# A decoder step whose second feed-forward takes its tokens as 256 and 320, with cache copies moved behind the weight loads

## The chip, the cores and the metric

The kernel runs on one core of a Trainium2 chip. The metric is the time of one execution in device microseconds; the median of three runs of the kernel before is 1784.57 us (1784.05 to 1786.42).

## What is computed

One layer of a hybrid decoder, for 1024 prompt tokens and 64 sample tokens (8 sequences of 8, each with 2048 cached rows of keys and values). Everything is float32.

```python
h = rmsnorm(x, norm_mix);  proj = h @ w_in                      # 1024 -> 3592
o_a = gated delta rule (4 heads of 128) on conv+silu of proj    # scratch mix, mixs[0]
o_b = dilated window attention (8 heads of 64)                  # prompt: own keys; sample: cache
x = x + concat(o_a, o_b) @ w_out                                # 1024 -> 1024
x = x + (silu(rmsnorm(x) @ w_gate) * (rmsnorm(x) @ w_up)) @ w_down   # 1024 -> 2816 -> 1024
y = rmsnorm(x, norm_final)
new_wk_sample = concat(cache_win_k, k)[:, 8:];  new_wv_sample = concat(cache_win_v, v)[:, 8:]
```

A sample query reads the cache at three strides: the last 512 rows (called near here), and before them rows 16 apart, of which 8 in every 16 are used, 96 groups of them (called far). The last line is a shift of the two caches by 8 rows: 8 x 2040 rows of 2 KB each, for keys and for values.

## The kernel before

Tokens stand in two groups: group 0 is 512 prompt tokens, group 1 the other 512; the 64 sample tokens go with group 0 up to attention and with group 1 from the second half of the output projection on (576 tokens then). Products of large matrices are made in three parts: an operand is split into a high part, rounded to a shorter float (`split`, L223 on ScalarE), and a low part, the rest (L224 on VectorE), and TensorE sums high x high, low x high and high x low (`mm`, L198).

A weight block of 0.5 MB is loaded by `wload` (L228, on the queue of the SyncE engine, SP) into one of `WB` = 2 buffers `wraw`; `wsplit` makes `whi` and `wlo` of it (three buffers each), or, where `own` is given, two tiles `own` of the caller's pool. `w_in`, `w_gate` and `w_up` are read as columns of 128 of the row-major matrix, runs of 512 B; `w_down` and `w_out` as runs of 1 or 2 KB.

The stages, in order of time: input norm and transposes (`norm_T`, L289 the scaled row, L294 the transposes; `wmix` is the norm's weight broadcast to all partitions, `ident` a part of the table `tab`), then `proj_a` and `proj_b` for both groups with the delta rule (`gdn`) beside them; first cache scores (`decode_k`), attention of group 0, and `outproj_a` (the half of the output projection that the delta rule feeds). Then the dense chain of group 0, `outproj_b(0)`, `ffn_norm(0)`, `ffn(0)`, runs beside three other works in turn: attention of group 1 (`attn(1)`), the rest of `decode_k`, and `decode_v` (cache values). At last comes the dense chain of group 1, `outproj_b(1)`, `ffn_norm(1)`, `ffn(1)`, which has nothing beside it but copies.

The work of a stage is written as generators that yield an estimate of their time, and `beside` takes steps of a side generator in proportion; a scheduler then orders each engine's instructions. What stands in an engine's order, or in a DMA queue, runs in that order.

`ffn` makes hidden blocks of 128 columns: `dense_T` for gate and for up (8 x 3 matmuls on `n` tokens each), tanh and product into `hh` and `hl`, and after 2 or 4 blocks the down product (`down`, `nat_mm`), which adds into `x2` (L1320). In `ffn(1)` the tokens stand as two pieces of 288; in `ffn(0)` as one of 512. The down product is 512 columns wide in `ffn(1)` and in the two-block step of `ffn(0)`, and 256 wide in the five four-block steps of `ffn(0)`. `outproj_b` works in four column pieces of 256 (L1238).

`decode_v` takes the sequences in pairs: the exponentials `Pd` (128 rows of both sequences by 616 columns) are transposed into `PT`, split into the tile `Z` at places that depend on the column group, and per sequence six loads `vt` (four far ones of 96 x 1024, two near ones of 128 x 1024, L1105) are split and multiplied: 26 matmuls of 512 columns a sequence.

The shifted caches are written in four ways. For keys: the near rows by eight copies of 1 MB from cache to output on the queue of GpSimd (POOL, L1026), written in `decode_k`; half of the far rows out of the loaded tile `kt` (L1039), half by `far_rows` (L1343), eight copies of 1.5 MB on SP beside `proj_b(0)`. For values: near and half of the far rows out of `vt` on POOL (L1108, L1110), the other half by `far_rows` beside the last dense chain.

Of the kernel before, what the change touches and what calls it, by code (L numbers as in the profile page):

```python
# [11 lines left out]
F32 = mybir.dt.float32  # L12
# [10 lines left out]
DB, DS = 8, 8  # L23
# [63 lines left out]
def consts():  # L87
# [6 lines left out]
    t["ident"] = p == c  # L94
# [43 lines left out]
    return off, {"table": table, "wb": wb, "dbias": np.ascontiguousarray(db_all), "xin": xin}  # L138


def laid_out(cache_k):

    k = cache_k[0, :, PAST - 512:].reshape(DB, 128, 4, 4, 128)
    return np.ascontiguousarray(k.transpose(0, 4, 3, 2, 1).reshape(DB, 128, 4, 512))


def body(tc, I, O, C, off):
# [25 lines left out]
    ident, ii, utri, ones = K("ident"), K("ii"), K("utri"), K("ones")  # L173
# [52 lines left out]
    def wload(src, k, n):  # L226
        raw = wp.tile([128, k, n], F32, name="wraw", tag="wraw", bufs=WB)
        sp.dma_start(raw, src)  # L228
        return raw

    def wsplit(src, k, n, raw=None, own=None):
        raw = wload(src, k, n) if raw is None else raw
        if own is None:
            hi = wp.tile([128, k, n], F32R, name="whi", tag="whi", bufs=WH)
            lo = wp.tile([128, k, n], F32R, name="wlo", tag="wlo", bufs=WL)
        else:
            hi, lo = (own.tile([128, k, n], F32R, name=f"own{q}", bufs=4) for q in range(2))
        split(hi, lo, raw)
        return hi, lo
# [80 lines left out]
    w_in = I["w_in"].rearrange("o (k p) n -> p (o k) n", p=128)  # L320
# [3 lines left out]
    def in_cols(i):  # L324
        return w_in[:, :, i * 128:(i + 1) * 128]
# [16 lines left out]
    def proj_a(G, tp, tb, hi, lo, ready={}):  # L342
# [38 lines left out]
        sp.dma_start(raw, w_in[:, :, 2048:2056])  # L381
# [35 lines left out]
    def proj_b(G, tp, hi, lo):  # L417

        W = GW[G]
        for kind in range(4):  # L420
            for j in range(4):
                c0_ = 2056 + kind * 512 + j * 128 if kind < 3 else 1536 + j * 128
                w = wsplit(w_in[:, :, c0_:c0_ + 128], 8, 128)
# [567 lines left out]
    def decode_k(tp, pairs, kb=2, kt_=3, qb=2, pb=1):  # L991
# [23 lines left out]
        for pi in pairs:  # L1015
            S = tp.tile([96, 2, 64], F32, name="S", tag="S", bufs=1)
            pa = obank()
            for s in range(2):
                b = 2 * pi + s
                c16, o16, c4, o4, src = cache_rows(I["cache_win_k"], O["new_wk_sample"], b)  # L1020
                for j in range(4):
                    for i in range(2):
                        hs = slice(i * 64, i * 64 + 64)
                        nc.gpsimd.tensor_copy(qbd[hs, s, j, 2 * j + i::8], qf[hs, j, b * 8:(b + 1) * 8])
                n = PAST - 512
                pool_q.dma_start(O["new_wk_sample"][0, b, n - DS:PAST - DS].rearrange("(a e) h d -> a (e h d)", a=64),  # L1026
                                 I["cache_win_k"][0, b, n:PAST].rearrange("(a e) h d -> a (e h d)", a=64))
# [31 lines left out]
    def decode_v(tp):  # L1059
# [6 lines left out]
        z = tp.tile([128, 13, 128], F32R, name="Z", bufs=1)  # L1066
        dve.memset(z.bitcast(F32), 0.0)
        X = tp.tile([128, 8, 64], F32, name="Xo", bufs=1)
        yield 3.0
        for pi in range(4):  # L1070
# [7 lines left out]
            pt = tp.tile([128, 6, 128], F32, name="PT", bufs=1)  # L1078
            p_ = abank()
            pe.transpose(p_[:96, 0:128], P[:, 0:96], ident)  # L1080
            pe.transpose(p_[:64, 128:256], pn, ident)
            act.activation(pt[:96, 0], p_[:96, 0:128], AF.Copy)
            act.activation(pt[:64, 1], p_[:64, 128:256], AF.Copy)
            p_ = abank()
            for i in range(4):
                pe.transpose(p_[:, i * 128:(i + 1) * 128], P[:, 96 + i * 128:224 + i * 128], ident)
            act.activation(pt[:, 2:6], p_.rearrange("p (i n) -> p i n", i=4), AF.Copy)
            for s in range(2):
                b = 2 * pi + s
                c = slice(s * 64, s * 64 + 64)  # L1090
                put = []
                for o in (0, 64):
                    put.append([bass.AP(tensor=z.tensor, offset=z.offset + o, ap=[[z.ap[0][0], 96], [136, 8], [1, 8]]),
                                z[:, 8:12, o:o + 64], z[:64, 12, o:o + 64]])
                srcs = [pt[:96, 0, c].rearrange("p (t h) -> p t h", t=8), pt[:, 2:6, c], pt[:64, 1, c]]
                for hi_, lo_, src_ in zip(*put, srcs):
                    split(hi_, lo_, src_)
                c16, o16, c4, o4, src = cache_rows(I["cache_win_v"], O["new_wv_sample"], b)
                po = obank()
                for i in range(6):  # L1100
                    n = 96 if i < 4 else 128
                    vt = tp.tile([128, 2, 512], F32, name="vt", tag="vt", bufs=TB)
                    vh = tp.tile([128, 2, 512], F32R, name="vh", bufs=VB)
                    vl = tp.tile([128, 2, 512], F32R, name="vl", bufs=VB)
                    sp.dma_start(vt[:n], c16[:96, 2 * i:2 * i + 2] if i < 4 else c4[:, 2 * i - 8:2 * i - 6])  # L1105
                    split(vh[:n], vl[:n], vt[:n])
                    if i < 4:
                        pool_q.dma_start(o16[0:95, 8 + 2 * i:10 + 2 * i], vt[1:96])  # L1108
                    else:
                        pool_q.dma_start(o4[:, 2 * i - 8:2 * i - 6], vt)  # L1110
                    for q in range(2):
                        mm(po, z[:n, 2 * i + q], vh[:n, q], i + q == 0, False)
                        mm(po, z[:n, 2 * i + q], vl[:n, q], False, False)
                    yield 2.5
                mm(po, z[:64, 12], vnh, False, False)
                mm(po, z[:64, 12], vnl, False, True)
# [28 lines left out]
    w_g = I["w_gate"].rearrange("o (k p) n -> p (o k) n", p=128)  # L1145
    w_u = I["w_up"].rearrange("o (k p) n -> p (o k) n", p=128)
    w_d = I["w_down"].rearrange("o (k p) n -> p (o k) n", p=128)
# [72 lines left out]
    def outproj_b(F, tp, x2):  # L1220
# [11 lines left out]
        for c in range(4):  # L1232
            w = wsplit(w_out[:, 4:8, c * 256:(c + 1) * 256], 4, 256)
            for i, rows, col in toks(F):
                ps = mbank()[:, :256]
                nat_mm(his(hi), his(lo), w, 4, rows, col, ps, True, True)
                xv = x2[:, col // 128, c * 256:(c + 1) * 256]
                dve.tensor_tensor(xv, ps, xv, op=OP.add)  # L1238
                yield 1.3
# [21 lines left out]
    def ffn(F, tp, x2, hp):  # L1261
        cols = [(0, 288), (288, 288)] if F else [(0, 512)]
# [19 lines left out]
        while f < nf:  # L1282
# [3 lines left out]
            for j in range(nb):  # L1286
                wg = wsplit(w_g[:, :, (f + j) * 128:(f + j + 1) * 128], 8, 128)
                wu = wsplit(w_u[:, :, (f + j) * 128:(f + j + 1) * 128], 8, 128)
                for c0, n in cols:
                    pg = yield from dense_T(*wg, hi, lo, c0, n)  # L1290
                    pu = yield from dense_T(*wu, hi, lo, c0, n)
                    th = hp.tile([128, 512], F32, name="hth", bufs=2)[:, :n]
                    act.activation(th, pg[:, :n], AF.Tanh, scale=0.5)  # L1293
                    dve.scalar_tensor_tensor(th, th, 1.0, pg[:, :n], op0=OP.add, op1=OP.mult)
                    dve.tensor_tensor(th, th, pu[:, :n], op=OP.mult)
                    act.activation(hh[j][:, c0:c0 + n], th, AF.Copy, scale=0.5)
                    m = min(n, 512 - c0)
                    dve.scalar_tensor_tensor(hl[j][:, c0:c0 + m], th[:, :m], 0.5, hh[j][:, c0:c0 + m].bitcast(F32),
                                             op0=OP.mult, op1=OP.subtract)
                    if m < n:  # L1300
                        dve.scalar_tensor_tensor(hh[j][:, 576:640], th[:, m:n], 0.5, hh[j][:, 512:576].bitcast(F32),
                                                 op0=OP.mult, op1=OP.subtract)
                yield 0.1
            last, wide = f + nb == nf, F or nb == 2
            ncol = 512 if wide else 256
            parts = nb * ncol // 1024

            def weights(c):

                k = nb // parts  # L1310
                return [wsplit(w_d[:, f + q * k:f + (q + 1) * k, c * ncol:(c + 1) * ncol], k, ncol, own=hp if F else None)
                        for q in range(parts)]
# [25 lines left out]

    def far_rows(c, o, new):
# [5 lines left out]
        sp.dma_start(o[0, :, PAST - DS:PAST].rearrange("b t h d -> b t (h d)"), new.rearrange("(b t) f -> b t f", t=DS))  # L1345

# [148 lines left out]
    far.run()  # L1495
# [28 lines left out]
```

## Time and profile before

| | before |
|---|---|
| median of three runs | 1784.57 us |
| the profiled execution | 1786.49 us |
| its span, first to last instruction | 1784.7 us |
| its mean granted TensorE clock | 0.981 of full speed |
| TensorE busy | 1697.0 us, 95% |
| VectorE busy | 1150.2 us, 64% |
| DMA | 324.96 MB, 182 GB/s over the span |

The profiled execution is 1.92 us above the median. Busy time counts the time from a matmul's start to its modelled end, and matmuls overlap, so that what one costs in a full stream is the distance from its start to the next start, not the duration in its row. The full clock is 2.4 GHz; a granted clock of 0.5 is 1.2 GHz.

### The profile page before, as it was taken

The page shows a single profiled execution, that of the slowest core. Times are in us where ns is not written, and L with a number is a line of the kernel's source. Part 1 is how long each engine was busy: PE and PEld are TensorE (multiplying, and loading weights), DVE is VectorE, ACT ScalarE, POOL GpSimd, SP SyncE. Part 2 cuts the span into 40 slices and gives each one's busy share as a digit, 9 for nine tenths or more (in the row PEclk, how much of TensorE's full clock was granted, in tenths as well). Part 3 has the DMA queues.
Part 4 walks back from the last instruction along what each step waited for, and adds up shares of the span by engine and source line. Part 5 has one row for each costly group of instructions (what it writes and reads, how often), then busy time and mean ns, then how long its engine had stood idle before and what let it go on. Part 6 is the DMA issues. An engine that isn't in the chain of part 4 may idle for free. (4 is left out here: it accounts for less than half of the span.)

```text
span 1784.7 us, 27958 instructions
## 1 busy us (share of the span) xinstructions
PE 1697.0 (95%) x10462; PEld 1464.7 (82%) x10462; DVE 1150.2 (64%) x2829; ACT 679.4 (38%) x1379; POOL 78.2 (4%) x200
## 2 busy tenths in 40 slices
PE   4999999997999999999999989999998999999997
PEld 4988789996766668878887778888887999999996
DVE  6978966866776757797666546676576444343435
ACT  4545434441423353676421134454234223131222
POOL 1000000001001000000011001111100000000000
PEclk9999999998999999999998999999998999999999
DMA  8645556468898867534299678798494333241321
GB/s 272 182 145 159 162 179 171 116 200 271 266 282 256 256 208 225 188 104 118 66 284 287 180 224 256 248 304 274 133 325 154 128 95 95 59 130 36 107 72 65
DMA packets 309569, 324.96 MB, mean 182 GB/s; under 512 B 28221, under 2 KB 260669, under 8 KB 307754
## 3 DMA queue, kind: packets, MB, share of 16 engines
q1 hardware_dynamic: 297754, 275.64, 51.6%
q0 software_dynamic: 10304, 43.08, 6.8%
q10 hardware_dynamic: 1376, 4.46, 0.7%
q8 instruction: 82, 1.34, 0.3%
q14 instruction: 53, 0.43, 0.1%
HBM read 251.31 MB, written 105.63 MB: 200 GB/s over the span
## 5 line engine op out<-in xcount | busy, mean ns | idle before, releaser
L198 PE MATMUL pm<-act_hi,whi 128*128 128x288 f32 (+1 forms) x1056 | 349.4, 331 | 0.2 <-ACT act_hi L223 0.2
L198 PE MATMUL pm<-act_lo,whi 128*128 128x288 f32 (+1 forms) x1056 | 348.1, 330 | 0.0
L198 PE MATMUL pm<-act_hi,wlo 128*128 128x288 f32 (+1 forms) x1056 | 347.4, 329 | 0.0
L223 ACT ACTIVATE whi<-wraw 128x1024 fp32r<-128x1024 f32 x182 | 192.8, 1059 | 381.8 <-PE pm L198 275.8
L224 DVE TENSOR_TENSOR wlo<-wraw,whi 128x1024 fp32r<-128x1024 f32 x182 | 222.3, 1222 | 123.8 <-ACT whi L223 123.3
L198 PE MATMUL pm<-xh,whi 128*128 128x320 f32 (+2 forms) x672 | 230.6, 343 | 11.5 <-ACT whi L223 8.6
L198 PE MATMUL pm<-xl,whi 128*128 128x320 f32 (+2 forms) x672 | 228.4, 340 | 0.1
L198 PE MATMUL pm<-xh,wlo 128*128 128x320 f32 (+2 forms) x672 | 226.7, 338 | 0.2
L198 PEld LDWEIGHTS pm<-act_hi,whi 128*128 128x128 f32 x1056 | 199.2, 189 | 18.4 <-issue 2.1
L198 PEld LDWEIGHTS pm<-act_hi,wlo 128*128 128x128 f32 x1056 | 199.3, 189 | 14.5 <-issue 0.5
L198 PEld LDWEIGHTS pm<-act_lo,whi 128*128 128x128 f32 x1056 | 199.3, 189 | 14.2 <-issue 0.2
L198 PEld LDWEIGHTS pm<-xh,whi 128*128 128x128 f32 x672 | 129.1, 192 | 25.9 <-ACT whi L223 9.1
L1320 DVE TENSOR_TENSOR x<-pm,x 128x256 f32<-128x256 f32 (+1 forms) x148 | 79.9, 543 | 98.2 <-PE pm L198 97.8
L198 PEld LDWEIGHTS pm<-xl,whi 128*128 128x128 f32 x672 | 129.0, 192 | 11.9 <-issue 3.2
L198 PEld LDWEIGHTS pm<-xh,wlo 128*128 128x128 f32 x672 | 128.7, 192 | 10.6 <-DVE wlo L224 1.5
L198 PE MATMUL pm<-own,hh 128*128 128x512 f32 x440 | 129.4, 390 | 0.0
L198 PE MATMUL pm<-whi,hh 128*128 128x256 f32 (+1 forms) x336 | 101.6, 303 | 12.9 <-DVE x L1320 7.6
L198 PE MATMUL pm<-whi,hl 128*128 128x256 f32 (+1 forms) x336 | 99.7, 299 | 0.0
L198 PE MATMUL pm<-wlo,hh 128*128 128x256 f32 (+1 forms) x336 | 99.4, 297 | 0.0
L198 PEld LDWEIGHTS pm<-own,hh 128*128 128x128 f32 x440 | 82.2, 188 | 16.9 <-issue 0.2
L198 PE MATMUL pm<-whi,nat_hi 128*128 128x256 f32 x288 | 83.4, 293 | 1.5 <-DVE n_ss L219 1.1
L1293 ACT ACTIVATE hth<-pm 128x288 f32<-128x288 f32 (+1 forms) x66 | 30.5, 462 | 139.4 <-PE pm L198 139.3
(362 smaller groups left out, 3180.9 us busy)
## 6 DMA issues: line engine op xcount, KB each, us to landing
wraw<-w_in SPq DMA_DIRECT2D x56, 512.0 KB, 4.6
wraw<-w_gate SPq DMA_DIRECT2D x44, 512.0 KB, 3.7
wraw<-w_up SPq DMA_DIRECT2D x44, 512.0 KB, 3.8
wraw<-w_down SPq DMA_DIRECT2D x44, 512.0 KB, 3.6
new_wk_sample<-cache_win_k SPq DMA_DIRECT2D x8, 1536.0 KB, 8.2
qbc<-smp SPq DMA_DIRECT2D x32, 384.0 KB, 7.2
kt<-cache_win_k SPq DMA_DIRECT2D x32, 384.0 KB, 7.0
vt<-cache_win_v SPq DMA_DIRECT2D x32, 384.0 KB, 4.2
```

The source lines that it names most:

```text
L198: pe.matmul(out, lhsT, rhs, start=start, stop=stop)
L223: act.activation(hi, src, AF.Copy)
L224: dve.tensor_sub(lo, src, hi.bitcast(F32))
L1293: act.activation(th, pg[:, :n], AF.Tanh, scale=0.5)
L1320: dve.tensor_tensor(xv, ps, xv, op=OP.add)
```

## The change

Seven edits.

1. The host lays the weights out in blocks, so that each of the 0.5 MB loads of `w_in`, `w_gate`, `w_up` and `w_down` reads 4 KB in one run per partition.
2. `ident` is loaded as a table of its own, behind `wmix`, and the rest of the table behind the five input tiles.
3. `move` issues one copy of 0.5 MB from cache to output on SP behind each weight load, as long as there are any. 16 such copies of near key rows start with the dense chain of group 0 and replace the eight of POOL; 64 of value rows (255 rows each, the whole shifted cache) start with the dense chain of group 1 and replace `far_rows` and the stores out of `vt`.
4. The far values come packed by the host, 128 rows full, three loads instead of four; the far exponentials are masked per residue and transposed as six full blocks, so that a sequence takes five loads and 22 matmuls, and a pair of sequences 11 transposes instead of 6. `Z` needs no clearing.
5. `outproj_b` works in two column pieces of 512, each with two loads of 0.5 MB.
6. All down products are 512 wide.
7. `ffn(1)` takes its tokens as 256 and 320. Its first two hidden blocks are made on the first 256 tokens, then on the other 320; the second block's weights go into `own` tiles meanwhile, with raw buffers (`raw2`) of their own.

```diff
+    moves = iter(())
+    def move():
+        x = next(moves, None)
+        if x is not None:
+            tc.keep_in_program_order(sp.dma_start(*(y.rearrange("s h d -> s (h d)") for y in x)))
+        return x
 def wload(src, k, n):
     raw = wp.tile([128, k, n], F32, name="wraw", tag="wraw", bufs=WB)
     sp.dma_start(raw, src)
+    move()
 def wsplit(src, k, n, raw=None, own=None):
+    if own is not None:
+        raw = own.tile([128, k, n], F32, name="raw2", bufs=2)
+        sp.dma_start(raw, src)
+        move()
...
-        return w_in[:, :, i * 128:(i + 1) * 128]
+        return I["w_in"][i]
...
 def decode_k(...):
-                pool_q.dma_start(O["new_wk_sample"][0, b, n - DS:PAST - DS]..., I["cache_win_k"][0, b, n:PAST]...)
...
 def decode_v(...):
-                for i in range(6):
+                for i in range(5):
-                    sp.dma_start(vt[:n], c16[:96, 2 * i:2 * i + 2] if i < 4 else c4[:, 2 * i - 8:2 * i - 6])
-                    split(vh[:n], vl[:n], vt[:n])
-                    if i < 4:
-                        pool_q.dma_start(o16[0:95, 8 + 2 * i:10 + 2 * i], vt[1:96])
-                    else:
-                        pool_q.dma_start(o4[:, 2 * i - 8:2 * i - 6], vt)
+                    sp.dma_start(vt, C["far_v"][b, i] if i < 3 else c4[:, 2 * i - 6:2 * i - 4])
+                    split(vh, vl, vt)
...
 def outproj_b(F, tp, x2):
-        for c in range(4):
-            w = wsplit(w_out[:, 4:8, c * 256:(c + 1) * 256], 4, 256)
+        for c in range(2):
+            w = [wsplit(w_out[:, k:k + 2, cs], 2, 512) for k in (4, 6)]
...
 def ffn(F, tp, x2, hp):
-        cols = [(0, 288), (288, 288)] if F else [(0, 512)]
+        cols = [(0, 256), (256, 320)] if F else [(0, 512)]
-            for j in range(nb):
+            early = F and f == 0
+            for j, (c0, n) in ([(j, c) for c in cols for j in range(nb)] if early else [(j, c) for j in range(nb) for c in cols]):
+                    ws[j] = [wsplit(I[x][f + j], 8, 128, own=hp if early and j else None) for x in ("w_gate", "w_up")]
-            last, wide = f + nb == nf, F or nb == 2
-            ncol = 512 if wide else 256
+            last, ncol = f + nb == nf, 512
...
     x0 = list(load_in(0, npl, range(2)))
-    sp.dma_start(tab, C["table"])
     wbc = bcast_row(npl, I["norm_mix"], "wmix")
+    sp.dma_start(ident, C["ident"])
     raws = [(i, wload(in_cols(i), 8, 128)) for i in IN_ORDER[:E1]]
     x0 += load_in(0, npl, range(2, 5))
+    sp.dma_start(tab, C["table"])
...
+    move_all(rows_of("cache_win_k", "new_wk_sample", PAST - 512, PAST, 256))
...
+    move_all(rows_of("cache_win_v", "new_wv_sample", DS, PAST, 255))
...
-    far = Side(far_rows(I["cache_win_v"], O["new_wv_sample"], smp[2]))
-    beside(out1, (far, 0.3))
-    beside(Side(ffn(1, op, x2, hp)), (far, 0.3))
+    beside(out1)
+    run(ffn(1, op, x2, hp))
```

Three places of the engines' orders show what these edits move. The first is the start of POOL's order, before and then changed; `gdn_S`, `Bz` and `N` are tiles of the delta rule.

```order
L1423 MEMSET gdn_S 128x512
L1026 DMA new_wk_sample<-cache_win_k 16x16384 x3
L1433 MEMSET Bz 128x1024
L1434 MEMSET N_1431 128x512
L1026 DMA new_wk_sample<-cache_win_k 16x16384 x3
```

```order
L1465 MEMSET gdn_S 128x512
L1475 MEMSET Bz 128x1024
L1476 MEMSET N_1433 128x512
L693 COPY N_1433<-L 32x4x32
L694 COPY N_1433<-L 32x4x32
```

The key copies, three of them right behind the first clearing, are gone from POOL. The second place is TensorE's order between `outproj_b(1)` (`nat_hi` its operand) and `ffn(1)` (`act_hi`, `act_lo` its operands, transposed from `xn`), before and then changed.

```order
L198 MATMUL pm<-wlo,nat_hi 128x256
L294 MATMUL pn<-tab,xn 128x128 x24
L198 MATMUL pm<-act_hi,whi 128x288 x2
L294 MATMUL pn<-tab,xn 128x128 x4
L198 MATMUL pm<-act_lo,whi 128x288
```

```order
L223 MATMUL pm<-wlo,nat_hi 128x512
L333 MATMUL pn<-ident,xn 128x128 x16
L223 MATMUL pm<-act_hi,whi 128x256
L223 MATMUL pm<-act_lo,whi 128x256
L223 MATMUL pm<-act_hi,wlo 128x256
```

A token tile of 128 has 8 transposes. Three tiles stood ahead of the first product, now two do; after 24 matmuls of 256 columns come the 16 transposes of tiles 2 and 3, after 14 more the 8 of the sample tile. The third place is SP's order at the start of `ffn(1)`, before and then changed; `wffn` and `wfin` are norm weights.

```order
L300 DMA wffn<-norm_ffn 128x1024
L1343 DMA new_wv_sample<-cache_win_v 96x4096
L228 DMA wraw<-w_gate 128x8x128
L228 DMA wraw<-w_up 128x8x128
L1343 DMA new_wv_sample<-cache_win_v 96x4096 x2
L228 DMA wraw<-w_gate 128x8x128
```

```order
L339 DMA wffn<-norm_ffn 128x1024
L253 DMA wraw<-w_gate 128x1024
L263 DMA new_wv_sample<-cache_win_v 16x8160
L253 DMA wraw<-w_up 128x1024
L263 DMA new_wv_sample<-cache_win_v 16x8160
L339 DMA wfin<-norm_final 128x1024
L269 DMA raw_13361<-w_gate 128x1024
```

A copy stands behind each of the first 58 of the 66 loads of `ffn(1)`; the other six of the 64 stand behind the two last loads of `ffn(0)` and the four of `outproj_b(1)`. SP's order up to attention of group 1 is otherwise the same as before, but for the table's place.

## Rows read from the trace of the kernel before

**Rows 1.** The page's part 1: busy us (share of the span) and count.
```profile
PE 1697.0 (95%) x10462; PEld 1464.7 (82%) x10462; DVE 1150.2 (64%) x2829; ACT 679.4 (38%) x1379; POOL 78.2 (4%) x200
```

**Rows 2.** Windows: us, busy (count) of each engine, granted clock, DMA share, GB/s.
```profile
0.00:18.00 18.00, 0.00 (x0) 0.00 (x0) 3.38 (x23) 3.58 (x5) 2.41 (x8) 1.00 0.89 318
...
884.00:902.00 18.00, 18.00 (x148) 17.72 (x148) 11.24 (x29) 3.74 (x4) 2.64 (x14) 1.00 0.61 177
...
900.00:1000.00 100.00, 93.17 (x482) 75.09 (x481) 63.77 (x80) 19.13 (x23) 13.96 (x43) 0.91 0.96 281
1040.00:1130.00 90.00, 82.10 (x439) 69.32 (x438) 52.62 (x78) 37.10 (x52) 10.86 (x22) 0.98 0.86 262
...
1316.00:1336.00 20.00, 20.00 (x172) 20.00 (x170) 15.63 (x44) 6.47 (x9) 0.00 (x0) 1.00 1.01 374
1336.00:1355.00 19.00, 10.11 (x50) 8.72 (x49) 17.75 (x49) 10.14 (x17) 0.95 (x1) 0.64 0.47 155
1362.00:1775.00 413.00, 413.00 (x2679) 388.58 (x2677) 181.57 (x315) 102.99 (x157) 0.00 (x0) 1.00 0.29 89
```

**Rows 3.** Timelines of DVE, POOL and SP at the start: start us, us, instruction.
```profile
17.23 1.28 DVE L289 SCALAR_TENSOR_TENSOR xn<-xt,n_ss,wmix 128x1024 f32<-128x1024 f32 x1 [8.97 <-DMA wmix<-norm_mix]
...
1.30 1.68 POOL L1026 DMA_DIRECT2D new_wk_sample<-cache_win_k  x3
...
1.66 0.43 SPq L1413 DMA_DIRECT2D tab<-table  x1
2.13 0.43 SPq L300 DMA_DIRECT2D wmix<-norm_mix  x1
```

**Rows 4.** Timeline of PE at the start.
```profile
23.05 0.56 PE L198 MATMUL pm<-xh,whi 128*128 128x256 f32 x1
...
28.02 1.65 PE L294 MATMUL pn<-tab,xn 128*128 128x128 f32 x12
...
34.45 1.09 PE L294 MATMUL pn<-tab,xn 64*128 64x64 f32 x8 [3.75 <-DVE n_ss L214]
```

**Rows 5.** Groups of PE by line and form: count | busy us, mean ns | idle before.
```profile
L198 PE MATMUL pm<-whi,hh 128*128 128x256 f32 x320 | 94.8, 297 | 12.8 <-DVE x L1320 7.6 <-DVE hth L1295 5.2
...
L198 PE MATMUL pm<-whi,nat_hi 128*128 128x256 f32 x288 | 83.4, 293 | 1.5 <-DVE n_ss L219 1.1 <-DVE xq L1210 0.3
```

**Rows 6.** Timeline of PE: streams of one form, first and last row.
```profile
904.64 0.39 PE L198 MATMUL pm<-act_hi,wlo 128*128 128x512 f32 x1
...
907.82 0.39 PE L198 MATMUL pm<-act_lo,whi 128*128 128x512 f32 x1
...
1335.76 0.28 PE L198 MATMUL pm<-wlo,nat_hi 128*128 128x256 f32 x1
...
1336.47 0.28 PE L198 MATMUL pm<-wlo,nat_hi 128*128 128x256 f32 x1
```

**Rows 7.** Timeline of PE: two transposes of `decode_v` with one matmul of 256 columns between them.
```profile
1169.41 0.27 PE L1080 MATMUL pa<-tab,Pd 128*96 128x128 f32 x1
...
1169.64 0.27 PE L1081 MATMUL pa<-tab,pn 128*64 128x128 f32 x1
```

**Rows 8.** Waits of SP's queue: us in total, times, longest; and PE's gap at 1061.
```profile
SPq L1105 <- DMA new_wv_sample<-vt: 45.6, 14, 8.6
...
1065.10 0.58 PE L198 MATMUL pm<-whi,hh 128*128 128x256 f32 x1 [3.85 <-DVE x L1320]
```

**Rows 9.** Timeline of PE between `outproj_b(1)` and `ffn(1)`.
```profile
1348.06 1.94 PE L294 MATMUL pn<-tab,xn 128*128 128x128 f32 x8 [3.39 <-DVE n_ss L216]
...
1353.40 0.59 PE L198 MATMUL pm<-act_hi,whi 128*128 128x288 f32 x1
```

**Rows 10.** The page's part 6, DMA issues: count, KB each, median us to landing.
```profile
wraw<-w_gate SPq DMA_DIRECT2D x44, 512.0 KB, 3.7
...
new_wv_sample<-cache_win_v SPq DMA_DIRECT2D x8, 1536.0 KB, 8.7
...
wb<-wb SPq DMA_DIRECT2D x8, 512.0 KB, 3.8
```

More of the change, by code (lines that the diff above doesn't have):

```diff
@@ L93, in consts @@
     t = {}
-    t["ident"] = p == c
     t["ii"] = (p % 64) == (c % 64)
@@ L171, in K @@
         return tab[:, o:o + n]
-    ident, ii, utri, ones = K("ident"), K("ii"), K("utri"), K("ones")
+    ident = cp.tile([128, 128], F32, name="ident")
+    ii, utri, ones = K("ii"), K("utri"), K("ones")
     hmask, bmask = K("hmask"), K("bmask")
@@ L1087, in decode_v @@
-            act.activation(pt[:, 2:6], p_.rearrange("p (i n) -> p i n", i=4), AF.Copy)
+            pf = tp.tile([128, 8, 96], F32, name="Pfar", bufs=1)
+            dve.tensor_tensor(pf, P[:, None, 0:96].to_broadcast([128, 8, 96]),
+                              bmask[:, :, None].to_broadcast([128, 8, 96]), op=OP.mult)
+            pfv = pf.rearrange("p t m -> p (t m)")
+            blocks = [pfv[:, k * 128:(k + 1) * 128] for k in range(6)]
+            blocks += [P[:, 96 + i * 128:224 + i * 128] for i in range(4)] + [pn]
@@ new lines, in decode_v @@
+            z = tp.tile([128, 11, 2, 2, 64], F32R, name="Z", bufs=1)
+            for k0 in range(0, 11, 4):
+                p_ = abank()
+                for k in range(k0, min(k0 + 4, 11)):
+                    n = 128 if k < 10 else 64
+                    pe.transpose(p_[:n, (k - k0) * 128:(k - k0 + 1) * 128], blocks[k], ident)
+                pv = p_.rearrange("p (k s n) -> p k s n", k=4, s=2)
+                if k0 < 8:
+                    split(z[:, k0:k0 + 4, :, 0], z[:, k0:k0 + 4, :, 1], pv)
+                else:
+                    split(z[:, 8:10, :, 0], z[:, 8:10, :, 1], pv[:, 0:2])
+                    split(z[:64, 10, :, 0], z[:64, 10, :, 1], pv[:64, 2])
@@ L1088, in decode_v @@
             for s in range(2):
                 b = 2 * pi + s
[L1090 to L1097, printed above, removed]
+                zk = [z[:, k, s].rearrange("p a n -> p (a n)") for k in range(11)]
@@ new lines, in ffn @@
+            ws = {}
+            for j, (c0, n) in ([(j, c) for c in cols for j in range(nb)] if early else [(j, c) for j in range(nb) for c in cols]):
+                if j not in ws:
+                    ws = ws if early else {}
+                    ws[j] = [wsplit(I[x][f + j], 8, 128, own=hp if early and j else None) for x in ("w_gate", "w_up")]
+                wg, wu = ws[j]
+                pg = yield from dense_T(*wg, hi, lo, c0, n)
+                pu = yield from dense_T(*wu, hi, lo, c0, n)
+                th = hp.tile([128, 512], F32, name="hth", bufs=2)[:, :n]
+                act.activation(th, pg[:, :n], AF.Tanh, scale=0.5)
+                dve.scalar_tensor_tensor(th, th, 1.0, pg[:, :n], op0=OP.add, op1=OP.mult)
+                dve.tensor_tensor(th, th, pu[:, :n], op=OP.mult)
+                act.activation(hh[j][:, c0:c0 + n], th, AF.Copy, scale=0.5)
+                m = min(n, 512 - c0)
+                dve.scalar_tensor_tensor(hl[j][:, c0:c0 + m], th[:, :m], 0.5, hh[j][:, c0:c0 + m].bitcast(F32),
+                                         op0=OP.mult, op1=OP.subtract)
+                if m < n:
+                    dve.scalar_tensor_tensor(hh[j][:, 576:640], th[:, m:n], 0.5, hh[j][:, 512:576].bitcast(F32),
@@ L1308, in weights @@
             def weights(c):
-                k = nb // parts
-                return [wsplit(w_d[:, f + q * k:f + (q + 1) * k, c * ncol:(c + 1) * ncol], k, ncol, own=hp if F else None)
-                        for q in range(parts)]
+                return [wsplit(I["w_down"][f // 2 + q, c], 2, 512, own=hp if F else None) for q in range(parts)]
             def down(tok, c, w):
@@ L1337, in ffn, with move_all @@
             f += nb
+    def move_all(m):
+        nonlocal moves
+        while move() is not None:
+            pass
+        moves = m
     def far_rows(c, o, new):
@@ L1345, in far_rows, with rows_of @@
         sp.dma_start(o[0, :, PAST - DS:PAST].rearrange("b t h d -> b t (h d)"), new.rearrange("(b t) f -> b t f", t=DS))
+    def rows_of(i, o, first, last, n):
+        for b in range(DB):
+            for r in range(first, last, n):
+                yield O[o][0, b, r - DS:r - DS + n], I[i][0, b, r:r + n]
     def steps(*gens):
@@ L1491, in body @@
     hp = pool(st0, "hh")
-    far = Side(far_rows(I["cache_win_v"], O["new_wv_sample"], smp[2]))
-    beside(out1, (far, 0.3))
-    beside(Side(ffn(1, op, x2, hp)), (far, 0.3))
-    far.run()
+    beside(out1)
+    sp.dma_start(O["new_wv_sample"][0, :, PAST - DS:PAST].rearrange("b t h d -> b t (h d)"),
+                 smp[2].rearrange("(b t) f -> b t f", t=DS))
+    run(ffn(1, op, x2, hp))
+    move_all(None)
     st0.close()
```

75 lines of the change are left out of this document (29 added, 46 removed).

## Prediction

> **What bounds the kernel now.** The page comes first: TensorE is busy 95% of the span [rows 1], so almost everything that TensorE doesn't have to do, or doesn't have to wait for, is time. The windows say where the other 5% are [rows 2]. In the last dense chain, from 1362 to 1775, it is busy 413 of 413 us at the full clock: nothing can be won there but columns. Between 1336 and 1355, where the second output projection passes into the second feed-forward, it is busy 10.11 of 19 us at 0.64 of the clock. From 1040 to 1130, the start of the cache values, it lacks 7.9 of 90 us, and from 900 to 1000, beside the cache scores, 6.8 of 100 us at a clock of 0.91, with the DMA engines at 0.96. In the first 18 us it does nothing. The timelines then say what each of these waits is for [rows 3, 4, 8, 9], the stream rows what a column costs [rows 6].
>
> The sum is made against the profiled execution, 1786.5 us, which is 1.9 us above the median of the runs. What a measurement of this kernel can tell from no change is about 0.2%, 3.6 us.
>
> **The start, -8.5 us.** The first scaled row (L289) starts at 17.23, after 8.97 us in which VectorE waits for `wmix` alone [rows 3]; its norm factor was there at 8.26. `wmix` is issued at 2.13, behind the table (0.53 MB) and with three copies of 1 MB that POOL issued at 1.30 [rows 3], and the engines move 318 GB/s in this stretch [rows 2]. The copies are gone and the table goes behind the inputs: 3.7 MB less ahead, 11.5 us at that rate, more than the wait. `wmix` should land at 7 to 8 us, and the row starts when its factor is there. What follows hangs on it in a chain (transposes, first product at 23.05 [rows 4]). Not more than 11, with a part of the 3.75 us gap at 34.45 [rows 4]; not less than 5, if the later input tiles come late instead. I take 8.5, since the factor's chain is then next. Later up to group 1's attention the engines' orders are the same, so this gain has nothing to be lost in.
>
> **Wider products, -9 us.** Five four-block steps of `ffn(0)` issue 960 matmuls of 256 columns (three groups of 320, one of them in [rows 5]) and `outproj_b` 416 (half of the 832 of the two projections: two groups of 288, one in [rows 5], and one of 256). They become 688 of 512. A stream of 512 goes at 3.18 us for 14 steps, 227 ns; one of 256 at 0.71 us for 6 steps, 118 ns [rows 6]; over 18 us of the down product, counting 146 whole ones, it is 123 ns [rows 2]. So a pair gains 9 to 19 ns, 688 pairs 6.5 to 13 us; I take 13 ns, 9 us. The Trainium skill ("TensorE: Matmul & The Clock Gate", the section on 56 against 53.3 ns) gives a full stream a fixed cost of about 2.5 ns a matmul; by it this term would be an estimated 1.7 us, and the rows, with 12 to 14 ns a matmul over the columns' time, speak for the larger one.
>
> **Packed values, -5 us.** Per sequence 22 matmuls of 512 instead of 26, 32 fewer in all, 7.3 us at 227 ns. A pair of sequences has 11 transposes instead of 6, 20 more; two stand 0.23 us apart with a matmul of 256 between [rows 7], which leaves 0.11 us for one, 2.2 us. The splits of eight loads (1.1 and 1.2 us each on ScalarE and VectorE) fall away too, beside TensorE's work. Ends: 4 and 6.
>
> **Stores out of `vt`, -5 us.** SP waits 45.6 us in all for these stores before it can load into a buffer again [rows 8], and weight loads queue behind it: the gap of 3.85 us at 1061 stands at the head of a down product whose weight was late [rows 8]. Without the stores, 20.5 MB less, the loads run on. The 7.9 us lacking from 1040 to 1130 and a clock of 0.98 (1.8 us) are the most that can come back; nothing comes back if VectorE's in-order queue is what holds the hidden blocks. I take half, 5.
>
> **The two early blocks, -7 us.** `outproj_b(1)` ends its matmuls at 1336.47 [rows 6]; the feed-forward's own stream starts at 1353.40 [rows 9]. In the 17 us lie 32 transposes (3.5 us at 0.11) and four products; the rest is the alternation of row scaling, transposes and splits on a clock at half level (0.64 in the mean [rows 2]). In the changed order the first product needs tiles 0 and 1 alone, and four gate and up products of 24 matmuls (11 us at 118 ns) stand between or behind the other tiles' transposes. Since the projection passes over all tokens in two rounds instead of four, tile 0 is also finished some 10 us ahead of the projection's end instead of 5 (a round's four tiles of 12 and one of 8 matmuls, 56 x 227 ns). Left over are the splits of tile 1 (two of 0.6 us on each engine) and some alternation. That the scheme works is seen at the start, where a product on 256 tokens begins at 23.05, ahead of the transposes of the next tiles at 28.02 [rows 4]. Ends: 2, if tiles 2 and 3 stall it as before, and 12.
>
> **Edits near nothing.** 256 + 320 columns are as many as 288 + 288, with as many matmuls: 0. The 4 KB runs: a load in 512 B runs lands in 3.7 us, one in 4 KB runs (`wb`) in 3.8 [rows 10], so nothing where TensorE waits for no load; from 900 to 1000, where the DMA engines are the bound, up to 14 us could come back and a less lucky order could cost 6; I take 1. The copies: 58 loads of the last chain drag 0.5 MB each. There are 66 loads in the 413 us of that chain, one in 6.3 us; load and copy are 1.05 MB, 2.8 us at the 374 GB/s that the engines moved from 1316 to 1336, when loads and far copies ran together [rows 2]. Prefetch by two raw and three split buffers covers that: 0, at worst 5. The 16 key copies go beside attention of group 1; its loads queue behind them, which is in these 5.
>
> Sum: 8.5 + 9 + 5 + 5 + 7 + 1 = 35.5 us, 1751.0 against the profiled execution, **1749.1** against the median.
>
> **The rivals.**
> (a) *The cache stages stay paced by their loads.* Then the stores' 5 us and the early blocks' next 5 don't come, the wider products gain 7, and the other order in 900 to 1000 costs 4: 8.5 + 7 + 5 + 2 - 4 = 18.5, **1766**. For it: the DMA share of 0.96 there, which the change hardly lowers (all eight key copies were issued by POOL long before). Against: the range from 1040 on loses its stores.
> (b) *The waits go altogether*: start 10, products 11, values 5, stores 9, early blocks 11, cache scores 10: 56, **1729**. For it: each is a wait for something that is removed or made shorter. Against: several have a second cause close behind.
> (c) *Copies starve the second feed-forward*, the side of slower. In a DMA queue things run in order; if a copy doesn't overlap with the next load, a load takes 3.7 plus at least a third of the 8.7 us of a copy of 1.5 MB [rows 10], 6.6 us against 6.3 had, which costs 58 x 0.3 = 20 us and leaves **1769**; if a copy of 0.5 MB takes 8.7 as well, 12.4 us and 58 x 6.1 = 356 us, **2105**. It decides from 6.3 + 35.5 / 58 = 6.9 us for load and copy. Against it: 374 GB/s with both in flight. The Trainium skill ("DMA: Bandwidth & Descriptors", anatomy of one DMA) speaks for it: about 2 us fixed and bytes at 436 GB/s for each transfer; by it load and copy one behind the other would take an estimated 6.4 us, no slower than the point above.
> (d) *The early blocks don't start early*, because the product still waits for all five tiles: 28.5, **1756**. Rows 4 speak against it.
>
> **Chances.** The forecast with (d), 1738 to 1759: 0.58. (a): 0.2. (b): 0.15. (c): 0.05, 0.04 of it slower; 0.02 are left for a loss that cancels the gains. The range from 1731 to 1767 takes in the forecast, (a) and the nearer half of (b). Faster 0.94, within 0.2% 0.02, slower 0.04.
>
> **What would show it.** Right: the first L289 row at about 8.5 us and its wait gone; streams of 227 ns in `ffn(0)`'s down products; no row for `vt` among SP's waits for stores; TensorE busy over 13 of the 19 us after `outproj_b(1)`; the last chain as full as before with the DMA share above 0.4. Wrong: gaps on TensorE in the last chain that end with a split behind `wraw` or `raw2` (then c), a first product of `ffn(1)` behind 32 transposes (d), or waits between 900 and 1000 longer than the 6.8 us (a).

## The result, and the profile after

The changed kernel takes 1987.0 us (1982.5 to 1990.3, four runs) against 1784.3 us: 1.113 times as long, with an interval of 1.110 to 1.116. The prediction was 1749.1 us (1731 to 1767), with 0.04 on slower. It was wrong in sign and in size.

The page of the kernel after, its first line and the 40 slices of TensorE and of its granted clock (in tenths):

```profile
span 1980.7 us, 26318 instructions
...
PE 1768.6 (89%) x9762; PEld 1472.2 (74%) x9762; DVE 1151.1 (58%) x2758; ACT 669.3 (34%) x1351; POOL 49.8 (3%) x144
...
PE   6999999989999998988999999978778878887888
PEclk9999999999999999988999999987889989898989
```

TensorE issues 700 matmuls fewer than in [rows 1] and is busy for 72 us more. The last third, full before, now has eights and sevens, with the clock below full: that is the place to look. The windows below give the same five stretches of the program for the changed kernel, cut at the same events: the start; from the end of the input projections to the end of the attention scores of group 1; from there to the last cache-value matmul; to the last transpose of the last normalisation; to the last matmul. The columns are the stretch, its length, then TensorE, its weight loads, VectorE, ScalarE, POOL, granted clock, DMA share and GB/s.

```profile
0.00:18.00 18.00, 6.29 (x26) 5.37 (x27) 11.00 (x51) 10.02 (x16) 0.72 (x5) 1.00 0.80 258
560.70:892.30 331.60, 304.29 (x1701) 231.21 (x1698) 228.19 (x653) 161.22 (x357) 8.51 (x27) 0.96 0.57 180
892.30:1254.70 362.40, 346.18 (x1516) 267.75 (x1516) 231.56 (x294) 125.14 (x156) 17.88 (x54) 0.98 0.66 207
1254.70:1394.84 140.14, 116.39 (x491) 90.64 (x489) 77.89 (x171) 39.32 (x57) 5.46 (x9) 0.87 0.37 129
1394.84:1971.37 576.53, 477.27 (x2690) 430.81 (x2690) 189.82 (x319) 105.35 (x162) 0.00 (x0) 0.92 0.31 112
```

The kernel before, same stretches (its start is in [rows 2]):

```profile
567.70:864.90 297.20, 287.63 (x1786) 225.28 (x1785) 225.96 (x663) 161.53 (x358) 8.53 (x27) 1.00 0.59 181
864.90:1264.30 399.40, 384.46 (x2103) 322.54 (x2102) 247.82 (x356) 139.45 (x190) 42.52 (x102) 0.97 0.79 239
1264.30:1361.33 97.03, 86.25 (x529) 75.16 (x527) 70.36 (x175) 36.80 (x54) 5.50 (x9) 0.93 0.67 233
1361.33:1775.27 413.94, 413.71 (x2680) 389.03 (x2680) 182.47 (x316) 103.66 (x159) 0.00 (x0) 1.00 0.30 90
```

At the last cache-value matmul the change is 9.6 us ahead (1254.7 against 1264.3). Then the last stage alone takes 162.6 us more: 99.3 us in which TensorE does nothing, and 63.6 us more of busy time for nearly the same work, on a mean clock of 0.92 instead of 1.00. The DMA engines are at 0.31 there, as before at 0.30: bandwidth isn't short.

What ends TensorE's idle time in that stage, from the chain of waits (engine and line that waits, what it waits for: us in total, times, longest):

```profile
ACT hth L1325 <- PE pm L223: 233.4, 43, 21.2
...
PE pm L223 <- ACT whi L248: 55.0, 32, 2.0
...
ACT own L248 <- DMA raw<-w_down: 28.1, 8, 6.0
PE pm L223 <- DVE wlo L249: 23.9, 37, 1.7
...
ACT whi L248 <- DMA wraw<-w_gate: 6.9, 4, 2.7
```

TensorE waits for the split of a weight. And that split seldom waits for its load: four times, 6.9 us in all, for `wraw` (the 28.1 us for down weights are 26.6 in a run below that copies nothing). One hidden block shows what it waits for, on ScalarE and then on TensorE:

```profile
1607.38 0.47 ACT L1328 ACTIVATE hh<-hth 128x320 fp32r<-128x320 f32 x1 [3.54 <-DVE hth L1327]
1607.75 1.04 ACT L248 ACTIVATE whi<-wraw 128x1024 fp32r<-128x1024 f32 x1
1614.39 0.38 ACT L1325 ACTIVATE hth<-pm 128x256 f32<-128x256 f32 x1 [5.59 <-PE pm L223]
1614.67 1.05 ACT L248 ACTIVATE whi<-wraw 128x1024 fp32r<-128x1024 f32 x1
```

```profile
1606.51 0.31 PE L223 MATMUL pm<-act_hi,wlo 128*128 128x320 f32 x1
1608.85 0.38 PE L223 MATMUL pm<-act_hi,whi 128*128 128x256 f32 x1 [2.03 <-ACT whi L248]
1609.07 0.28 PE L223 MATMUL pm<-act_lo,whi 128*128 128x256 f32 x1
1610.11 0.58 PE L223 MATMUL pm<-act_hi,wlo 128*128 128x256 f32 x1 [0.76 <-DVE wlo L249]
1610.48 0.41 PE L223 MATMUL pm<-act_hi,whi 128*128 128x256 f32 x1
1610.70 0.41 PE L223 MATMUL pm<-act_lo,whi 128*128 128x256 f32 x1
...
1613.78 0.28 PE L223 MATMUL pm<-act_hi,whi 128*128 128x256 f32 x1
1613.90 0.28 PE L223 MATMUL pm<-act_lo,whi 128*128 128x256 f32 x1
...
1615.77 0.39 PE L223 MATMUL pm<-act_hi,whi 128*128 128x256 f32 x1 [1.48 <-ACT whi L248]
```

The split of the gate weight (1607.75) starts the moment the previous block's `hh` is done, and has no idle time of its own: the data lay in `wraw`, and the split stood behind `hh` in ScalarE's list. The split of the up weight (1614.67) stands behind the tanh of its own block, which needs the whole gate product. So this block pays 2.03 + 0.76 + 1.48 us and a few tenths, and behind the first two gaps matmuls of 256 columns start 0.22 us apart (1610.48, 1610.70), at a granted clock of 0.50 from 1610.48 to 1613.05, instead of 0.12 (1613.78, 1613.90) at the full clock. SP, meanwhile, issues nothing from 1598.91 to 1629.76:

```profile
1597.92 0.95 SPq L269 DMA_DIRECT2D raw<-w_down  x1
1598.91 0.56 SPq L263 DMA_DIRECT2D new_wv_sample<-cache_win_v  x1
1629.76 0.33 SPq L269 DMA_DIRECT2D raw<-w_down  x1
```

The third load of a down weight waits for a `raw2` buffer, thus for a split that stands behind the block's work. From 1606 us until that load nothing is in flight, and the buffers wait for a list.

### The profile page after: what moved, and what is told of

Read it like the earlier page. It is cut to its first block, busy times and chain, and to the rows that moved or that the text cites. A ratio compares the mean times of both kernels' runs of the same rounds, so it can differ in the third digit from the quotient of the medians.

```text
span 1980.7 us, 26318 instructions
## 1 busy us (share of the span) xinstructions
PE 1768.6 (89%) x9762; PEld 1472.2 (74%) x9762; DVE 1151.1 (58%) x2758; ACT 669.3 (34%) x1351; POOL 49.8 (3%) x144
## 4 chain that ended last, share of the span: by engine, by line
PE 63%; DVE 11%; DMA 5%; ACT 4%; issue 2%; SPq 0%; DVEq 0%; ACTq 0%
PE pm L223 48%; PE po L223 5%; DVE wlo L249 4%; DMA kt<-cache_win_k 2%; PE ps L223 2%; PE pg L223 2%; ACT whi L248 2%; PE pa L937 1%; PE pc L223 1%; PE pa L223 1%; DVE pl L249 1%; DMA wraw<-w_in 1%; DVE hth L1327 1%; ACT hh L1328 0%; DMA wraw<-w_up 0%
## 5 line engine op out<-in xcount | busy, mean ns | idle before, releaser
L223 PE MATMUL pm<-act_hi,whi 128*128 128x512 f32 (+2 forms) x1024 | 360.6, 353 | 61.8 <-ACT whi L248 58.0
L223 PE MATMUL pm<-act_hi,wlo 128*128 128x512 f32 (+2 forms) x1024 | 360.9, 352 | 26.7 <-DVE wlo L249 26.7
L223 PE MATMUL pm<-act_lo,whi 128*128 128x512 f32 (+2 forms) x1024 | 355.1, 347 | 0.1
L223 PEld LDWEIGHTS pm<-act_hi,whi 128*128 128x128 f32 x1024 | 211.8, 207 | 88.3 <-ACT whi L248 66.4
L1349 DVE TENSOR_TENSOR x<-pm,x 128x512 f32<-128x512 f32 x108 | 74.4, 690 | 116.8 <-PE pm L223 116.6
L1326 DVE SCALAR_TENSOR_TENSOR hth<-hth,pm 128x256 f32<-128x256 f32 (+2 forms) x66 | 35.0, 530 | 144.4 <-ACT hth L1325 144.4
L1327 DVE TENSOR_TENSOR hth<-hth,pm 128x256 f32<-128x256 f32 (+2 forms) x66 | 35.1, 531 | 144.1 <-PE pm L223 144.0
L1325 ACT ACTIVATE hth<-pm 128x256 f32<-128x256 f32 (+2 forms) x66 | 30.9, 468 | 243.7 <-PE pm L223 243.7
L1328 ACT ACTIVATE hh<-hth 128x256 fp32r<-128x256 f32 (+2 forms) x66 | 33.2, 503 | 192.9 <-DVE hth L1327 192.8
L223 PE MATMUL pm<-whi,nat_hi 128*128 128x256 f32 (+1 forms) x216 | 71.8, 340 | 7.8 <-ACT whi L248 5.9
```

The source lines that it names most:

```text
L223: pe.matmul(out, lhsT, rhs, start=start, stop=stop)
```

## The experiments

Theory **T1**: the order of the engines' lists is planned ahead by a scheduler, and with copies in SP's queue it plans the loads late, so that each split is put behind the previous block's work; on the chip the data is there, and the list is what costs. **T2**: the copies' traffic, or a load that stands behind a copy in the queue, is what costs. **T3**: another of the seven edits. Counted back from its end, ScalarE's list of before has the next block's gate weight split when the tanh of a block's first piece comes up; the changed kernel's list has that block's own up weight still to split. "Last stage" below is the fifth stretch above.

**No copies.** Both calls of `move_all` that hand copies out are removed.

> The changed kernel without the 80 copies of cache rows (the far rows of both new caches are left out). Theory T1 (the copies on SP's queue make the order of the engines be planned with each weight split behind the previous block's work; on the chip that order is what costs): 1740 to 1760 us, since without copies ScalarE's list has a split ahead of its block again. T2 (the copies' own traffic delays the loads): the same 1740 to 1760. T3 (another part of the change, such as the 256/320 pieces, the early blocks' buffers or the separate raw buffers of the down weights, makes the splits late): still above 1930.

1749.35 us (1746.4 to 1752.3), 0.978 of before (0.975 to 0.982). T3 falls: no other edit makes the splits late. The trace, same five stretches:

```profile
0.00:18.00 18.00, 5.22 (x21) 4.29 (x22) 9.96 (x40) 9.89 (x15) 0.72 (x5) 1.00 0.76 234
559.30:862.30 303.00, 290.98 (x1695) 222.31 (x1694) 226.63 (x655) 161.65 (x359) 8.57 (x27) 0.99 0.57 178
862.30:1206.10 343.80, 340.64 (x1521) 265.80 (x1521) 228.59 (x292) 122.79 (x154) 17.81 (x54) 1.00 0.66 210
1206.10:1326.25 120.15, 110.82 (x529) 89.29 (x527) 83.75 (x179) 44.57 (x64) 5.46 (x9) 0.97 0.46 151
1326.25:1737.56 411.31, 411.31 (x2653) 386.60 (x2653) 178.69 (x312) 99.69 (x155) 0.00 (x0) 1.00 0.24 76
```

Against it the changed kernel loses 48.6 us up to the last cache-value matmul (1254.7 against 1206.1), 20.0 us up to the last transpose and 165.2 us in the last stage, together the 234 us between the two spans.

**The late order alone, no copies** (edit shortened).

```diff
-    ws[j] = [wsplit(I[x][f + j], ...) for x in ("w_gate", "w_up")]
+    ws[j] = [wsplit(I["w_gate"][f + j], ..., pin=late)]
     pg = yield from dense_T(*ws[j][0], hi, lo, c0, n)
+    act.activation(th, pg[:, :n], AF.Tanh, scale=0.5)
+    ws[j].append(wsplit(I["w_up"][f + j], 8, 128, pin=True))   # pin: ScalarE's half kept in program order
```

> No copies at all (the far rows of both new caches are left out), but the second feed-forward's splits pinned on ScalarE so that its list reads as in the changed kernel: the gate weight's split behind the previous block's last hh, the up weight's behind the tanh of its own block, the down weights' behind the last block. T1: slow without any copy traffic, 1930 to 1980 us, with gaps near 2 us ahead of a gate product in each block. T2: 1745 to 1775, a few us above the kernel without copies. T3: as T1, so this run tells T1 from T2 only.

1874.4 us (1870.2 to 1881.0). The number misses T1's range and lies far from T2's. The range was set as if the whole loss lay in this stage. In the stage itself:

```profile
1317.34:1859.14 541.80, 456.60 (x2633) 414.71 (x2632) 186.32 (x313) 102.24 (x158) 0.00 (x0) 0.92 0.18 60
```

```profile
PE pm L223 <- ACT whi L248: 60.0, 35, 2.0
```

Block for block ScalarE's list reads as the changed kernel's here, and the stage takes 541.8 against 411.3 us, with the changed kernel's clock (0.92) and its wait for `whi` (60.0 against 55.0 us), and not a byte copied. The order alone is 130.5 of the 165.2 us of this stage.

**Half the bytes.** Each copy carries 127 rows (`y[0:127]`).

> Every copy is pinned behind its load as in the changed kernel, but carries 127 rows instead of 255 or 256, so half the bytes (half of the far rows are left out). ScalarE's list in the second feed-forward still has the splits late, from the third block on. T1: nearly as slow as the changed kernel, 1930 to 1985 us. T2: half of the loss or less, 1840 to 1880. T3: as T1.

1809.5 us (1808.1 to 1814.6). It misses T1's range and goes below T2's. The last stage is 461.8 us at a clock of 0.99. The list of this kernel was read too coarsely: counted at the first tanh its splits are as late as the changed kernel's, but from a group's second block on the next gate weight is split ahead of the block's last `hh`, not behind it, and only the first block behind a down product waits. So this run changed the order along with the bytes, and doesn't tell T1 from T2.

**Copies from ScalarE's queue**, not pinned (`act.dma_start`).

> All copies, whole, issued from ScalarE's queue and not pinned, so that they stand spread over its list and the splits stand early again. T1: the loss is gone, 1745 to 1775 us; some may be lost where a copy meets the stages whose DMA engines are full. T2: the same 32 MB and 8 MB still collide with loads, above 1850. T3: above 1930.

2006.1 us (1993.4 to 2008.3): T1's range is missed, and the time lies in those of T2 and T3. The last copy goes out at 1288 us, so the last stage has none beside it and is full (411.33 of 411.33 us). The loss is spread over the stages ahead (in the first 560 us TensorE is busy for 444.9, against 525.0 without copies), whose lists are all in another order. Why it costs so much there was not followed up. With the copies beside other stages and every list changed, the run can't tell T2 from a bad order.

**Copies from POOL's queue, each behind its load** (edit shortened).

```diff
-            tc.keep_in_program_order(sp.dma_start(...))
+            y = tc.keep_in_program_order(nc.gpsimd.dma_start(...))
+            tc.add_manual_dep(y.ins, load.ins.name, Sync)    # starts when its load has landed
```

> All 80 copies, whole, issued from POOL's queue instead of SP's, each made to wait until the load that it stood behind has landed, so that they are spread in time as in the changed kernel, with the same bytes. ScalarE's list in the second feed-forward then has each split one block ahead again. T1 (the planned order is what costs): 1745 to 1765 us, the stage behind the last normalisation near 411 us as without copies. T2 (the traffic costs): above 1850, that stage above 500 us.

1757.1 us (1742.1 to 1759.5), 0.981 of before (0.976 to 0.986). All 40 MB are copied, and the last stage is that of the kernel without copies, so T2 falls for the bytes in this stage:

```profile
1336.51:1747.83 411.32, 411.32 (x2653) 386.57 (x2653) 178.75 (x311) 99.70 (x155) 23.80 (x49) 1.00 0.42 144
```

```profile
ACT whi L248 <- PE pm L223: 90.7, 39, 2.5
```

The wait has changed sides: the split now waits for TensorE to give a buffer free, where TensorE waited for the split. A copy in this stage takes 5.3 us from issue to landing, longer than the 4.9 us in the changed kernel, and it costs TensorE nothing. Of the 10.3 us by which this span is longer than that without copies, 7.5 are there at the end of the input projections (566.8 against 559.3), ahead of the first copy.

**Copies on SP as in the change, early order.** The splits are traced up to a block ahead, and ScalarE's and VectorE's work of the second feed-forward is kept in that order (edit shortened, comments added):

```diff
+    pg = yield from dense_T(*got["w_gate", f + j], hi, lo, c0, n)
+    if c0: fetch()          # next block's gate weight: load and split
+    pu = yield from dense_T(*got["w_up", f + j], hi, lo, c0, n)
...
+    if c0: fetch()          # next block's up weight
+    keep(act.activation(hh[j][:, c0:c0 + n], th, AF.Copy, scale=0.5))
```

> The changed kernel with all copies on SP's queue behind their loads, untouched; only the second feed-forward's splits and the work on ScalarE and VectorE around them are traced up to a block ahead and pinned in that order. The first part of the program is as in the changed kernel. T1: the stage behind the last normalisation falls from 576 us to 412 to 440 us, the whole to 1825 to 1860 us (what is lost before the end of the cache values, some 48 us, and in the second output projection, some 20 us, stays). T2 in the form that a load stands in SP's queue behind a copy and comes late: that stage stays above 540 us, the whole above 1945 us.

1840.3 us (1833.7 to 1854.1), as T1 has it:

```profile
1387.74:1822.58 434.84, 422.40 (x2691) 394.42 (x2690) 184.49 (x319) 104.58 (x162) 0.00 (x0) 0.99 0.40 149
```

The same copies in the same queue behind the same loads, and the last stage falls from 576.5 to 434.8 us. What is left over 411.3, 23.5 us, is the most that the queue can cost in this execution, the fastest of the four (1833.7); part of it is the order written here, which puts four splits of down weights in front of a tanh.

**Key copies alone** (the second `move_all` is removed).

> Only the 16 copies of key rows behind loads of the first dense chain beside the attention of group 1; the 64 copies of value rows are left out. T1 and T2 alike: the 48 us by which the changed kernel reaches the end of the cache values later than the kernel without copies stay (1790 to 1805 us), the second feed-forward is as without copies (near 411 us). If the two losses were not separate, the time is near 1750 or near 1900.

1801.1 us (1797.8 to 1806.7). The two losses are separate: the last cache-value matmul ends at 1256.6 as in the changed kernel, and the last stage takes 411.33 us.

**An eighth of the bytes**, all copies in their places (`y[0:31]`).

> The 80 copies stand pinned behind their loads in SP's queue, in the same number, with 31 rows instead of 255 or 256 each (seven eighths of the far rows are left out). The splits in the second feed-forward stand one block ahead again. T1: 1745 to 1765 us. T2 by bytes: an eighth of the loss, 1775 to 1785. By a cost for each copy, whatever its size: near the changed kernel, above 1930.

1740.9 us (1739.0 to 1743.2), 4 us below T1's range and 8 below the kernel without copies. That there are 80 more transfers in SP's queue, pinned, costs nothing. Where the 8 us come from was not followed up; the last stage takes 411.2 us as without copies, and the lists ahead of it differ.

**All copies late on POOL:** the keys too behind loads of the second feed-forward, as 8 copies of 1 MB ahead of the 64.

> As the kernel with its copies paced on POOL's queue, but the key copies too behind loads of the second feed-forward (8 copies of 1 MB, then the 64 of value rows, one behind each load that has one now). T1: with nothing added beside the attention of group 1, 1742 to 1756 us; the last stage stays at 411 us even with 40 MB copied beside it. T2 by bytes: the last stage grows above 425 us.

1752.4 us (1748.3 to 1759.1, six runs), 0.982 of before (0.979 to 0.984). In the last stage 33 MB of the copies go out, the DMA engines are at 0.47, and TensorE is busy all the time:

```profile
1328.27:1739.60 411.33, 411.33 (x2653) 386.57 (x2653) 178.49 (x311) 99.70 (x155) 27.58 (x57) 1.00 0.47 156
```

The other copies go out ahead of it, beside the second output projection.

**Copies on SP, not pinned** (no `keep_in_program_order`).

> The changed kernel with its copies on SP's queue, but free to be placed by the scheduler. ScalarE's list has the splits ahead in the first five blocks of the second feed-forward and late from the sixth on. T1 (the order that is planned when copies stand in SP's queue): still slow, 1860 to 1960 us, the first five blocks full. If it is the pins that cost: near 1750.

1889.8 us (1885.0 to 1898.9), in T1's range, last stage 513.6 us. The pins alone aren't the cause: 102 of the 165 us of the last stage stay without them, since copies that the scheduler places as it likes on SP still make it put the splits late. Key copies go out from 34 us on here, and the input projections end at 591 us, 32 later than without copies.

**Copies on POOL, held to nothing.**

> All copies on POOL's queue and not held to a load, so that they go out in two bursts, 16 and 58 of 0.5 MB, as fast as POOL can issue them. The order of the splits is the early one. T1: 1750 to 1790 us, with a dent where the bursts fill the DMA engines (30 MB at about 370 GB/s are 80 us) and a full last stage behind it. T2: above 1850.

1785.0 us (1779.1 to 1793.1), no change from before (0.998 to 1.003). Here traffic does cost:

```profile
1340.00:1400.00 60.00, 50.59 (x318) 48.20 (x317) 23.00 (x37) 12.14 (x19) 16.07 (x34) 0.89 1.00 348
```

While the burst lasts the DMA engines are full and TensorE lacks 9.4 of 60 us; the last stage is 433.6 us, 22.3 more than with paced copies, and from the end of the input projections to the last cache-value matmul it takes 662 us against 647. The whole is 28 us slower than with copies paced on the same queue, and 202 faster than the change, where they stand on SP.

**Copies paced on POOL, tokens as 288 + 288, no early blocks.**

> The kernel with copies paced on POOL's queue, with the second feed-forward's tokens as 288 and 288 again and no blocks begun early. The prediction's term for the early blocks was 7 us (2 to 12); the trace without copies shows about 5 between the second projection's last product and the same point of the feed-forward. So 1760 to 1766 us against 1757 with them.

1752.7 us (1750.3 to 1758.7): the range is missed, and the time is not above the 1757.1 with them. From the last cache-value matmul to the last matmul it takes 537.2 us against 533.9 with early blocks. These 3.3 us are from one trace of each, and less than the two programs differ by ahead of this point.

## Why the prediction was wrong

**The other terms came out in the sum.** Without copies the kernel takes 1749.35 us, where 1749.1 stood for everything with the copies at 0. That they agree to a quarter of a microsecond is luck: the early blocks brought less than was forecast, and the kernel with an eighth of the copied bytes is 8 us faster still. By its steps:

- The start, -8.5: in the changed kernel the first scaled row starts at 7.66 us without a wait, against 17.23 in [rows 3], and in the kernel without copies the input projections end 8.4 us earlier (559.3 against 567.7). In the other runs that have the same start and no copies beside it they end between 554.0 and 566.8, so the size of the term is known to some 6 us only.

```profile
7.66 1.28 DVE L328 SCALAR_TENSOR_TENSOR xn<-xt,n_ss,wmix 128x1024 f32<-128x1024 f32 x1
```

- Wider products, -9: the down products of `ffn(0)`, now 512 columns wide, start 227 ns apart in a full stream, as was forecast. Against 118 to 123 for 256 columns a pair gains 9 to 19 ns, and 688 pairs some 9 us; the term was not measured by itself. The fixed cost of about 2.5 ns a matmul in the Trainium skill ("TensorE: Matmul & The Clock Gate", the section on 56 against 53.3 ns) would make it an estimated 1.7 us; the streams of this kernel, 12 to 14 ns a matmul over the columns' time at the full clock, don't agree with it.
- Packed values, stores out of `vt`, cache scores, with the wider products and part of the early blocks, were forecast as 20 to 27 us together. From the projections' end to the last transpose it is 793.6 us before and 767.0 without copies, 26.7 less. How they share it was not tried; steps this small are near what any new order of the lists brings (8 us between the kernels with none and with an eighth of the copies).
- Early blocks, -7 (2 to 12): 3.3 us by one trace of each. The first product starts behind 16 transposes, as planned, but TensorE still waits for the norm factor of the second tile (in the kernel without copies):

```profile
1311.02 1.94 PE L333 MATMUL pn<-ident,xn 128*128 128x128 f32 x8 [6.32 <-DVE n_ss L241]
```

**The step that failed** is one sentence: "Prefetch by two raw and three split buffers covers that: 0, at worst 5." It took from the buffers that the loads would run ahead. But how far ahead a split stands is not set by buffers alone: it is written in ScalarE's list before the run, and the change altered this list. The copies, put at 0, cost 238 us (1987.0 against 1749.35). Some 49 of them come with the key copies, which the next sentence of the prediction counts in the same 5. 165.2 are lost in the last stage, where the order explains 130.5 by itself, and the early order with the copies untouched removes 141.7. Rival (c) had the right side and place, but the wrong mechanism: it priced a load and a copy that follow each other in a queue, decided by 6.9 us for both. Copies in the changed kernel land in 4.9 us and DMA engines stand idle two thirds of the stage. The figures that (c) takes from the Trainium skill ("DMA: Bandwidth & Descriptors", anatomy of one DMA) are given there for transfers that GpSimd issues, and these copies were issued by SP. The rival's price of 20 us at a load of 6.6 us is near what the queue may still cost (23.5 us at most). The test that the prediction named, gaps in the last chain that end with a split behind `wraw`, is met, while its meaning was different: the split waited for its turn.

It could have been seen ahead: the lists of the two kernels were there to be compared on ScalarE. The prediction looked at SP's, which the edit names, and argued the consumers from [rows 2], where the chain was full.

**What stays open.** The 49 us ahead of the cache values' end come with the key copies on SP (one run has them alone). The bytes alone don't cost them: with the same copies on POOL, behind the same loads, it is 647.1 us from the end of the input projections to the last cache-value matmul, against 646.8 without copies and 694.0 in the changed kernel. That they too are a matter of order fits, but no run fixed the order there with the copies in place, and a load that stands behind a copy in SP's queue is not ruled out: with the key copies alone three splits wait 17.4 us there for loads of `w_gate`, and TensorE's own waits there have many causes. The 20 us in the second output projection are open in the same way. And what the scheduler reckons for a copy is only inferred, from the lists that come out with half and with an eighth of the bytes.

## What to carry to other kernels

Where a scheduler writes each engine's order ahead of the run, a transfer added to a busy queue can change the lists of the engines that use what this queue loads: compare the consumers' lists, not only the queue's, and ask how many steps ahead of its use each operand is made. A wait of TensorE for a split that itself waited for nothing is the mark of an order that is too late, and bandwidth was not short there (DMA share 0.31). The bulk copies did best here on a queue on which little else is planned, each held to a load that is paced already: with all of them late on POOL the kernel is 1.8% faster than before and 11.8% faster than the change.

## What was not expected of the hardware

33 MB copied beside the last feed-forward cost TensorE nothing as long as they came one by one (DMA share 0.47, no idle time), while 30 MB sent at once, at 348 GB/s with the loads, cost 22 us. And gaps cost more than their length: in the last stage of the changed kernel 99 us of idle time, in gaps of at most 2.7 us, brought 64 us more of busy time with them. Most of it is the clock: a mean of 0.92, on levels of 1.0 and 0.5, is about a sixth of the stage at the half level, by an estimate from these numbers 46 us.
